# Conformer/attention encoder layer on one core: branches stored as two halves, score products chunk by chunk, and the convolution norm in seventeen short steps

## The chip, the cores and the metric

One core of a Trainium2 chip runs the whole kernel in one launch. The metric is the device time of one launch in microseconds (us). The profile is one execution taken by the hardware profiler; its times are counted from the first instruction of that execution.

## The reference, cut to what matters

One encoder layer, on a prompt of 1024 tokens and a sample of 256 tokens, which the kernel lays side by side as T = 1280 columns (features on the 128 partitions, in blocks of 128). Everything is float32.

```
h = modulate(rms_norm(x), sh1, sc1)                       # sh, sc, g: from silu(c) @ w_ada + b_ada
c_q, c_kv, k_r, conv_in, sg_in, gate_in = split(h @ w_in)
y_attn = attention(c_q, c_kv, k_r) @ w_attn_o             # 8 heads, softmax over all keys of the sequence
y_conv = silu(layer_norm(depthwise_conv31(glu(conv_in)))) @ w_conv_o    # 512 channels
y_sg   = (u * (spatial mix of layer_norm(v))) @ w_sg_o                  # 512 channels
x = x + g1 * ((ga*y_attn + gc*y_conv + gs*y_sg) @ w_out)  # ga, gc, gs = sigmoid(gate_in)
x = x + g2 * conv_ffn(modulate(rms_norm(x), sh2, sc2))
```

The layer norm of the convolution branch runs over 512 channels, that is over four blocks of 128 partitions. Its mean and its variance are sums over partitions, made on TensorE by products with a matrix of ones.

## The kernel before, in words

**Products.** Nearly all products are made three times, from operands split into a high part (`hi`, rounded to fp32r) and a low part (`lo`, the rest): hi times hi, hi times lo, lo times hi (`mm3`, line 130). `to_hi` (L117) makes the high part on GpSimd (POOL in the profile), `to_lo` (L120) subtracts on VectorE (DVE). `split` (line 142) does both on a [128, 1280] tile. Weights are loaded by SyncE (SP), split by the same two engines, and held up to three jobs ahead (`run_jobs`).

**Jobs and side steps.** The work is a list of jobs, each of which writes its instructions in program order. Beside them runs a queue `side` of short steps; `run_side(n)` writes the next n of them between two jobs. A scheduler then sorts each engine's instructions: it takes them in program order as they become ready by its own estimate, so an engine with nothing ready may take up later work, and an instruction that is ready goes ahead of everything later in the program. On the chip each engine, and each queue of transfers (SP's and POOL's), then runs strictly in the order that came out.

**The stretch around the change.** 24 gate jobs (`gate`, line 640), each one block of `h @ w_in` with a sigmoid on ScalarE (ACT, L643) and a store to `gate_d`. Behind gate 16 the side queue is emptied; then it gets the convolution norm as one step (`conv_norm`, line 322) and the 16 blocks of conditioning (`ada_steps`: start, `ada_blk` 0 to 15 on VectorE at L663, end). Behind each of the gates 17 to 23 run three side steps, 19 in all. `end_one` writes what is left, gives the tiles of `h` back, and attention follows (`attention`, line 747): it takes four output tiles `ob`, then loads head 0 with `load_head` (five transfers of 640 KB on POOL's queue, L726 and L729: q hi, q lo, k hi, k lo, v), and then goes through 72 units of scores (L736), softmax (L741 to L744), transposes (L801) and products with v (L818). Each next head is loaded two units into the head before; in head 7 the place of the next head is taken by `branch_load(us_d)`, which loads the four blocks of the gated branch and splits them. After attention come 24 jobs `branch_out`, and with the second of these `branch_load(cn_d)`, the same for the convolution branch. Both branches were stored to DRAM as they are, one tile per block: `us_d` by `sgu` (L421), `cn_d` by `conv_norm` (L350).

**The norm as one step.** `conv_norm` loads the four blocks (L326), adds them (L328 on POOL, L329 and L330 on DVE), makes the mean in three column chunks with a product by ones (L333, tile `pcm`) and subtracts it out of PSUM on DVE (L335, twelve instructions); then squares (L337 to L340), variance (L344, tile `pcv`), `rsqrt_big` (L149 and L151 to L154 on DVE, L150 on ACT), and for each block a product with the inverse (L348, every second one on POOL), silu (L349) and a store. The pool `sm` that holds `pcm` and `pcv` has two buffers.

**The slots.** All big tiles (1280 columns) come from 33 slots. The list of free slots is first in, first out, fixed when the program is written, and each slot is a buffer of its own:

```
def take(self, dt=F32, w=SLOTW):
    i = self.free.popleft()
    ...
    t = self.pool.tile([P, w], dt, name=f"t{self.n}", tag=f"s{i}")
def drop(self, *ts):
    ...
        self.free.append(i)
```

The first instruction that writes a newly taken tile waits until the last one that read or wrote the tile that had the slot before is done; where that was a store, until the store has landed.

## Time and profile before

| what | value |
|---|---|
| median of 3 runs | 2137.91 us (2137.29 to 2138.53) |
| the profiled execution, its own time | 2137.02 us |
| its span, first to last instruction | 2135.3 us |
| TensorE (PE) busy | 2076.5 us, 97% of the span |
| VectorE (DVE) busy | 1447.7 us, 68% |
| ScalarE (ACT) busy | 821.3 us, 38% |
| GpSimd (POOL) busy | 601.8 us, 28% |
| mean granted TensorE clock | 0.992 of full |

How to read it: an engine's time is the time in which one of its instructions runs. The rows of a timeline give the start in us, the duration in us, engine, line of the kernel, operation, the tiles written and read, the number of instructions merged into the row, and in square brackets how long the engine sat idle just before and what ended that. A row `DMA_DIRECT2D` under SP or POOL is the issue of a transfer; its landing is shown apart. A merged row runs from the start of its first instruction to the end of its last.

### The profile page before, as it was taken

How to read it: one execution, taken by the hardware profiler on the slowest of the kernel's cores; microseconds unless marked ns; L12 is line 12 of the kernel's file. 1: busy time of each engine (PE TensorE's matmuls, PEld its weight loads, DVE VectorE, ACT ScalarE, POOL GpSimd, SP SyncE). 2: the span in 40 equal slices, each digit the busy share in tenths (PEclk: the TensorE clock that was granted, in tenths of full speed). 3: DMA queues.
4: the chain of work that ended last, by engine and by line, in shares of the span. 5: the costliest groups of instructions: out<-in, count | busy, mean ns of one | idle time of the engine just before them, and what ended most of it. 6: DMA issues, size and time to landing. Idle time of an engine off the chain costs nothing. (4 is left out here: it accounts for less than half of the span.)

```text
span 2135.3 us, 29511 instructions
## 1 busy us (share of the span) xinstructions
PE 2076.5 (97%) x11094; PEld 1768.9 (83%) x11094; DVE 1447.7 (68%) x2151; ACT 821.3 (38%) x1637; POOL 601.8 (28%) x460
## 2 busy tenths in 40 slices
PE   6999999999999999999999998999999999999999
PEld 2888888887887788887888877888888888788889
DVE  6969798545447588888786398766666666644344
ACT  5110130345433177762000165544444444533233
POOL 2302202232312144452133432444444443000000
PEclk9999999999999999999999999999999999999999
DMA  8102232457685733326635322232223323856455
GB/s 340 49 23 80 91 112 83 144 176 223 186 278 181 233 104 113 106 100 254 216 139 193 106 99 71 95 96 95 84 85 94 94 84 104 261 176 199 136 172 162
DMA packets 146544, 300.82 MB, mean 141 GB/s; under 512 B 12129, under 2 KB 69601, under 8 KB 146401
## 3 DMA queue, kind: packets, MB, share of 16 engines
q1 hardware_dynamic: 136032, 254.37, 35.5%
q0 software_dynamic: 10368, 44.57, 6.7%
q8 instruction: 87, 1.43, 0.3%
q14 instruction: 57, 0.46, 0.1%
HBM read 220.24 MB, written 78.64 MB: 140 GB/s over the span
## 5 line engine op out<-in xcount | busy, mean ns | idle before, releaser
L1125 PE MATMUL b<-t,wq 128*128 128x512 f32 (+1 forms) x2904 | 551.9, 352 | 9.2 <-ACT t L1045 4.2
L1125 PEld LDWEIGHTS b<-t,wq 128*128 128x128 f32 x2904 | 474.9, 190 | 86.6 <-ACT t L1045 4.6
L139 PE MATMUL pb<-t,whi 128*128 128x512 f32 (+1 forms) x1632 | 443.4, 358 | 0.0
L120 DVE TENSOR_TENSOR wq<-wst,wq 128x512 fp32r<-128x512 f32 x308 | 247.4, 812 | 182.4 <-ACT wq L989 181.0
L139 PEld LDWEIGHTS pb<-t,whi 128*128 128x128 f32 x1632 | 289.2, 190 | 41.4 <-POOL whi L117 0.2
L1249 PE MATMUL pd<-t,wq 128*128 128x512 f32 (+1 forms) x1584 | 302.9, 354 | 0.0
L1249 PEld LDWEIGHTS pd<-t,wq 128*128 128x128 f32 x1584 | 261.7, 189 | 41.2
L989 ACT ACTIVATE wq<-wst 128x512 fp32r<-128x512 f32 x308 | 193.0, 630 | 260.1 <-PE pd L1249 70.5
L139 PE MATMUL pb<-t,wlo 128*128 128x512 f32 (+1 forms) x816 | 290.7, 356 | 0.0
L117 POOL TENSOR_SCALAR whi<-wst 128x1024 fp32r<-128x1024 f32 (+1 forms) x76 | 96.3, 1267 | 412.1 <-PE pb L139 184.7
L139 PE MATMUL bp<-t,whi 128*128 128x512 f32 x640 | 200.3, 393 | 2.9 <-DVE t L120 2.9
L120 DVE TENSOR_TENSOR t<-t,t 128x512 fp32r<-128x512 f32 (+4 forms) x139 | 135.0, 992 | 89.6 <-ACT t L1208 67.0
L294 DVE SCALAR_TENSOR_TENSOR t<-t,col,t 128x1009 f32<-128x1009 f32 (+14 forms) x240 | 194.2, 876 | 0.0
L139 PEld LDWEIGHTS pb<-t,wlo 128*128 128x128 f32 x816 | 154.8, 190 | 21.2
L120 DVE TENSOR_TENSOR wlo<-wst,whi 128x1024 fp32r<-128x1024 f32 (+1 forms) x76 | 82.4, 1086 | 113.6 <-POOL whi L117 103.3
L139 PEld LDWEIGHTS bp<-t,whi 128*128 128x128 f32 x640 | 118.8, 189 | 27.5 <-DVE t L120 4.1
L139 PE MATMUL bp<-t,wlo 128*128 128x512 f32 x320 | 125.1, 391 | 0.0
L736 PE MATMUL ps<-t,t 128*128 128x512 f32 (+1 forms) x432 | 113.6, 396 | 4.0 <-ACT t L742 2.5
L117 POOL TENSOR_SCALAR t<-t 128x1280 fp32r<-128x1280 f32 (+3 forms) x37 | 79.2, 2151 | 135.0 <-DMA t<-in_wqkv 59.9
L1183 POOL TENSOR_TENSOR t<-t,t 128x1280 f32<-128x1280 f32 x22 | 73.4, 3335 | 155.7 <-ACT wq L989 116.1
L744 POOL TENSOR_SCALAR t<-t,sz 128x1024 f32<-128x1024 f32 (+1 forms) x80 | 82.4, 1030 | 119.4 <-DVE sz L743 107.8
L643 ACT ACTIVATE t<-pb 128x1280 f32<-128x1280 f32 x24 | 29.8, 1243 | 206.6 <-PE pb L139 199.5
(198 smaller groups left out, 2870.8 us busy)
## 6 DMA issues: line engine op xcount, KB each, us to landing
wst<-in_wup SPq DMA_DIRECT2D x66, 512.0 KB, 3.6
wst<-in_wdn SPq DMA_DIRECT2D x132, 256.0 KB, 2.9
t<-in_ada SPq DMA_DIRECT2D x48, 512.0 KB, 6.3
qk_d<-t SPq DMA_DIRECT2D x80, 256.0 KB, 3.3
t<-qk_d POOLq DMA_DIRECT2D x32, 640.0 KB, 4.7
wst<-in_win SPq DMA_DIRECT2D x36, 512.0 KB, 4.1
gate_d<-t SPq DMA_DIRECT2D x24, 640.0 KB, 3.3
t<-gate_d SPq DMA_DIRECT2D x24, 640.0 KB, 5.3
```

Source lines behind the costliest of these rows:

```text
L117: G.tensor_scalar(out=out, in0=in_, scalar1=1.0, scalar2=0.0, op0=ALU.mult, op1=ALU.add)
L120: V.tensor_tensor(out=out, in0=in_, in1=hi.bitcast(F32), op=ALU.subtract)
L139: PE.matmul(ps.at(o, n) if isinstance(ps, Two) else ps[:, o:o + n], ws[:, c:c + P], ms[:, s:s + n], start=first and j == 0 and q == 0, sto ...
L294: V.scalar_tensor_tensor(out=ac[:, o + a:o + e], in0=ci[:, o + a + d:o + e + d], scalar=w, in1=ac[:, o + a:o + e], op0=ALU.mult, op1=ALU.add)
L643: S.activation(out=gt, in_=ps[:, :T], func=AF.Sigmoid)
L736: PE.matmul(ps[:, o + c:o + c + w], qk[a][:, q0:q0 + P], qk[b][:, k0 + c:k0 + c + w], start=q == 0, stop=q == 2)
L744: G.tensor_scalar(out=pr[:, o:o + n], in0=pr[:, o:o + n], scalar1=z[:, 2:3], scalar2=0.0, op0=ALU.mult, op1=ALU.add)
L989: S.activation(out=w[:, :HB], in_=src, func=AF.Copy)
L1125: PE.matmul(ps, w[:, c + k * P:c + (k + 1) * P], bs[k][i], start=start and k == 0 and q == 0, stop=stop and k == 3 and q == 2, skip_group_ ...
L1183: G.tensor_tensor(out=c["y1"], in0=c["y1"], in1=y2, op=ALU.mult)
L1249: PE.matmul(pss[m][:, :n], w[:, a + m * P:a + (m + 1) * P], t[:, b:b + n], start=k == 0 and q == 0, stop=k == KF - 1 and q == 2)
```

## The change

- `us_d` and `cn_d` get a second plane. `sgu` splits its result at once (`put`: POOL to_hi, DVE to_lo, two stores instead of one). `conv_norm` makes the two halves at its end, the high one on ACT. `branch_load` then only loads eight tiles, on POOL's queue instead of SP's, and splits nothing.
- `scores` goes chunk by chunk (512 keys): the three products of a chunk one behind the other, instead of both chunks for each of the three.
- `conv_norm` no longer writes instructions at once. It hands 17 steps to the side queue: load, sums, mean of three chunks, centre of four blocks, squares, variance of three chunks, four blocks. The first sum moves from POOL to DVE; the mean goes from PSUM to SBUF by an ACT copy and is then subtracted from whole blocks; the four products with the inverse are all on DVE.
- The order behind gate 16 is turned round: first the conditioning (18 steps with start and end), then the norm (17 steps). Five side steps instead of three run behind each of the gates 17 to 23, 35 in all. The last five, behind gate 23, are the variance of the third chunk and the four blocks.

```diff
@@ -104,9 +104,9 @@
         return col[:, at + i:at + i + n]
 
     gate_d = dr.tile([3, KD, P, T], F32, name="gate_d")
-    us_d = dr.tile([4, P, T], F32, name="us_d")
+    us_d = dr.tile([4, 2, P, T], F32, name="us_d")
     ac_d = dr.tile([4, P, T], F32, name="ac_d")
-    cn_d = dr.tile([4, P, T], F32, name="cn_d")
+    cn_d = dr.tile([4, 2, P, T], F32, name="cn_d")
     lat_d = dr.tile([NT, P, 6 * P], F32, name="lat_d")
     qk_d = dr.tile([2, 2, H, P, T], F32, name="qk_d")
     v_d = dr.tile([H, P, NT, P], F32, name="v_d")
@@ -144,6 +144,12 @@
         to_hi(h[:, :width], src[:, :width])
         to_lo(l[:, :width], src[:, :width], h[:, :width])
         return h, l
+
+    def put(dst, src):
+        hl = split(src)
+        for p in range(2):
+            SY.dma_start(dst[p], hl[p].bitcast(F32))
+        sl.drop(*hl)
 
     def rsqrt_big(y, ps, o, n, scale, s, t):
         V.tensor_scalar(out=s[:, o:o + n], in0=ps, scalar1=scale, scalar2=EPS, op0=ALU.mult, op1=ALU.add)
@@ -320,36 +326,60 @@
         job(lambda: run_side(n))
 
     def conv_norm():
-        acc = []
-        for b in range(4):
-            acc.append(sl.take())
-            SY.dma_start(acc[b], ac_d[b])
-        t1, t2 = sl.take(), sl.take()
-        G.tensor_tensor(out=t1, in0=acc[0], in1=acc[1], op=ALU.add)
-        V.tensor_tensor(out=t2, in0=acc[2], in1=acc[3], op=ALU.add)
-        V.tensor_tensor(out=t1, in0=t1, in1=t2, op=ALU.add)
-        for o, n in CH3:
+        acc, t, u = [], [], []
+
+        def load():
+            for b in range(4):
+                acc.append(sl.take())
+                SY.dma_start(acc[b], ac_d[b])
+            t.extend((sl.take(), sl.take()))
+
+        def sums():
+            V.tensor_tensor(out=t[0], in0=acc[0], in1=acc[1], op=ALU.add)
+            V.tensor_tensor(out=t[1], in0=acc[2], in1=acc[3], op=ALU.add)
+            V.tensor_tensor(out=t[0], in0=t[0], in1=t[1], op=ALU.add)
+
+        def mean(o, n):
             ps = sm.tile([P, 512], F32, name="pcm", tag="sm")
-            PE.matmul(ps[:, :n], ones, t1[:, o:o + n], start=True, stop=True)
-            for b in range(4):
-                V.scalar_tensor_tensor(out=acc[b][:, o:o + n], in0=ps[:, :n], scalar=-1.0 / 512,
-                                       in1=acc[b][:, o:o + n], op0=ALU.mult, op1=ALU.add)
-        S.activation(out=t1, in_=acc[0], func=AF.Square)
-        for b in range(1, 4):
-            S.activation(out=t2, in_=acc[b], func=AF.Square)
-            V.tensor_tensor(out=t1, in0=t1, in1=t2, op=ALU.add)
-        y, t3 = sl.take(), sl.take()
-        for o, n in CH3:
+            PE.matmul(ps[:, :n], ones, t[0][:, o:o + n], start=True, stop=True)
+            S.activation(out=t[1][:, o:o + n], in_=ps[:, :n], func=AF.Copy, scale=1.0 / 512)
+
+        def centre(b):
+            V.tensor_tensor(out=acc[b], in0=acc[b], in1=t[1], op=ALU.subtract)
+
+        def squares():
+            S.activation(out=t[0], in_=acc[0], func=AF.Square)
+            for b in range(1, 4):
+                S.activation(out=t[1], in_=acc[b], func=AF.Square)
+                V.tensor_tensor(out=t[0], in0=t[0], in1=t[1], op=ALU.add)
+
+        def var(o, n):
+            if not u:
+                u.extend((sl.take(), sl.take()))
             ps = sm.tile([P, 512], F32, name="pcv", tag="sm")
-            PE.matmul(ps[:, :n], ones, t1[:, o:o + n], start=True, stop=True)
-            rsqrt_big(y, ps[:, :n], o, n, 1.0 / 512, t2, t3)
-        sl.drop(t1, t2, t3)
-        for b in range(4):
-            (G if b % 2 else V).tensor_tensor(out=acc[b], in0=acc[b], in1=y, op=ALU.mult)
+            PE.matmul(ps[:, :n], ones, t[0][:, o:o + n], start=True, stop=True)
+            rsqrt_big(u[0], ps[:, :n], o, n, 1.0 / 512, t[1], u[1])
+
+        def block(b):
+            if b == 0:
+                sl.drop(*t, u.pop())
+            V.tensor_tensor(out=acc[b], in0=acc[b], in1=u[0], op=ALU.mult)
             S.activation(out=acc[b], in_=acc[b], func=AF.Silu, scale=cv("clg", b), bias=cv("clb", b))
-            SY.dma_start(cn_d[b], acc[b])
-            sl.drop(acc[b])
-        sl.drop(y)
+            h_, l_ = sl.take(F32R), sl.take(F32R)
+            S.activation(out=h_, in_=acc[b], func=AF.Copy)
+            to_lo(l_, acc[b], h_)
+            SY.dma_start(cn_d[b, 0], h_.bitcast(F32))
+            SY.dma_start(cn_d[b, 1], l_.bitcast(F32))
+            sl.drop(acc[b], h_, l_)
+            if b == 3:
+                sl.drop(u.pop())
+
+        side.extend((load, sums))
+        side.extend([lambda c=c: mean(*c) for c in CH3])
+        side.extend([lambda b=b: centre(b) for b in range(4)])
+        side.append(squares)
+        side.extend([lambda c=c: var(*c) for c in CH3])
+        side.extend([lambda b=b: block(b) for b in range(4)])
 
 
     wv, vg = [], []
@@ -418,7 +448,7 @@
                 scalar=cv("sgg", g), in1=tt[:, g * P:(g + 1) * P].unsqueeze(1).to_broadcast([P, NT, P]),
                 op0=ALU.mult, op1=ALU.add)
             V.tensor_tensor(out=us, in0=us, in1=u, op=ALU.mult)
-            SY.dma_start(us_d[g], us)
+            put(us_d[g], us)
             sl.drop(us, u)
             if g == 3:
                 sl.drop(wst, tt, *vg)
@@ -705,10 +735,10 @@
             job(lambda: run_side(4))
         elif j == 16:
             job(lambda: run_side(len(side)))
-            job(lambda: side.append(conv_norm))
             job(lambda: ada_steps(range(16)))
+            job(conv_norm)
         else:
-            job(lambda: run_side(3))
+            job(lambda: run_side(5))
 
     def end_one():
         run_side(len(side))
@@ -730,9 +760,9 @@
         return r, t
 
     def scores(ps, o, qk, q0, k0, n):
-        for q, (a, b) in enumerate(((0, 2), (0, 3), (1, 2))):
-            for c in range(0, n, 512):
-                w = min(512, n - c)
+        for c in range(0, n, 512):
+            w = min(512, n - c)
+            for q, (a, b) in enumerate(((0, 2), (0, 3), (1, 2))):
                 PE.matmul(ps[:, o + c:o + c + w], qk[a][:, q0:q0 + P], qk[b][:, k0 + c:k0 + c + w],
                           start=q == 0, stop=q == 2)
 
@@ -845,10 +875,10 @@
     def branch_load(src):
         r = []
         for b in range(4):
-            st = sl.take()
-            SY.dma_start(st, src[b])
-            r.append(split(st))
-            sl.drop(st)
+            hl = sl.take(F32R), sl.take(F32R)
+            for p in range(2):
+                G.dma_start(hl[p], src[b, p])
+            r.append(hl)
         return r
 
     job(attention)
```

## Rows read from the trace of the kernel before

**Rows 1.** The page's first lines: the span, and TensorE's busy time with its share of the span and the number of its instructions, products and weight loads.

```profile
span 2135.3 us, 29511 instructions
PE 2076.5 (97%) x11094; PEld 1768.9 (83%) x11094; DVE 1447.7 (68%) x2151; ACT 821.3 (38%) x1637; POOL 601.8 (28%) x460
```

**Rows 2.** The timeline of DVE, PE and ACT in the stretch of the gates 17 to 23: the sum of the four blocks, the three mean products, and the sigmoids at the ends of the gates 17, 18, 22 and 23.

```profile
624.77 1.49 DVE L330 TENSOR_TENSOR t<-t,t 128x1280 f32<-128x1280 f32 x1
...
645.25 1.88 PE L333 MATMUL pcm<-t,ones 128*128 128x512 f32 x4
652.68 1.12 PE L333 MATMUL pcm<-t,ones 128*128 128x256 f32 x2 [2.34 <-DVE t L335]
...
645.45 1.24 ACT L643 ACTIVATE t<-pb 128x1280 f32<-128x1280 f32 x1 [12.43 <-PE pb L139]
...
665.66 1.24 ACT L643 ACTIVATE t<-pb 128x1280 f32<-128x1280 f32 x1 [2.13 <-PE pb L139]
...
723.14 1.24 ACT L643 ACTIVATE t<-pb 128x1280 f32<-128x1280 f32 x1 [12.54 <-PE pb L139]
736.92 1.24 ACT L643 ACTIVATE t<-pb 128x1280 f32<-128x1280 f32 x1 [12.53 <-PE pb L139]
```

**Rows 3.** Busy time by stretch, two pieces of 5 us behind the mean products: from left the stretch, its length, busy us and instructions of PE, of its weight loads, DVE, ACT and POOL, the granted clock, the DMA share and GB/s.

```profile
650.00:655.00 5.00, 2.66 (x8) 1.85 (x7) 5.00 (x10) 0.00 (x0) 0.00 (x0) 0.78 0.86 313
655.00:660.00 5.00, 5.00 (x21) 4.04 (x20) 2.83 (x6) 3.01 (x3) 0.00 (x0) 0.88 0.05 21
```

**Rows 4.** The timeline where attention starts: the end of a conditioning block (DVE), the first of head 0's loads (POOL), the first scores (PE) and the first softmax (ACT).

```profile
705.36 0.23 DVE L665 TENSOR_SCALAR ada<-ada,col 128x2 f32<-128x2 f32 x1
...
705.84 0.60 POOL L726 DMA_DIRECT2D t<-qk_d  x1 [9.21 <-DVE ada L665]
...
738.21 3.06 PE L736 MATMUL ps<-t,t 128*128 128x512 f32 x12 [1.33 <-ACT t L643]
743.77 4.49 PE L736 MATMUL ps<-t,t 128*128 128x512 f32 x12 [2.50 <-ACT t L742]
...
741.21 1.28 ACT L742 ACT_TABLE_LOAD   x1 [3.06 <-DVE sz L741]
```

**Rows 5.** The timeline of DVE and ACT in the norm itself: the addition of a square on 1280 columns, a 256-column step of the inverse root, the two table loads, the inverse root on ACT, and the four silus.

```profile
663.57 1.49 DVE L340 TENSOR_TENSOR t<-t,t 128x1280 f32<-128x1280 f32 x1 [1.34 <-ACT t L339]
...
674.47 0.42 DVE L151 SCALAR_TENSOR_TENSOR t<-t 128x256 f32<-128x256 f32 x1
...
668.89 1.28 ACT L150 ACT_TABLE_LOAD   x1 [1.99 <-DVE t L149]
670.18 1.46 ACT L150 ACTIVATE t<-t 128x512 f32<-128x512 f32 x3
671.66 1.28 ACT L349 ACT_TABLE_LOAD   x1
682.23 5.63 ACT L349 ACTIVATE t<-t,col 128x1280 f32<-128x1280 f32 x4 [9.28 <-POOL t L348]
```

**Rows 6.** Transfers of one 640 KB tile, all of the kernel: what is moved, the issuing queue, count, size and median us from issue to landing.

```profile
us_d<-t SPq DMA_DIRECT2D x4, 640.0 KB, 3.1
cn_d<-t SPq DMA_DIRECT2D x4, 640.0 KB, 5.3
t<-us_d SPq DMA_DIRECT2D x4, 640.0 KB, 5.4
t<-qk_d POOLq DMA_DIRECT2D x32, 640.0 KB, 4.7
```

**Rows 7.** The same from 595 to 760 us only, head 0's and head 1's v; and, as busy time by stretch (columns as in rows 3), the 5 us from 595 to 745 us in which the transfers were fastest, while `cn_d` was stored.

```profile
t<-v_d POOLq DMA_DIRECT2D x2, 640.0 KB, 7.2
685.00:690.00 5.00, 5.00 (x23) 4.13 (x22) 4.97 (x5) 4.96 (x5) 3.36 (x2) 1.00 1.00 403
```

**Rows 8.** The timeline of attention's end: PE at the ninth unit of the heads 5, 6 and 7, DVE's splits of the gated branch, and the transposes that came after them.

```profile
903.56 0.53 PE L736 MATMUL ps<-t,t 128*128 128x256 f32 x3
...
931.93 0.52 PE L736 MATMUL ps<-t,t 128*128 128x256 f32 x3
...
965.55 0.52 PE L736 MATMUL ps<-t,t 128*128 128x256 f32 x3
...
942.34 6.12 DVE L120 TENSOR_TENSOR t<-t,t 128x1280 fp32r<-128x1280 f32 x3
...
950.25 1.11 PE L801 MATMUL ptt<-ident,t 128*128 128x128 f32 x4 [4.16 <-DVE t L779]
```

**Rows 9.** The timeline of the gated branch (`sgu`), 172 to 246 us: a weight's high half on POOL twice, and DVE waiting for one; then the last split of the weights that the next stage needs, and ACT's first instruction of that stage. Last, the whole stretch 174 to 240 us (columns as in rows 3).

```profile
204.94 6.00 POOL L117 TENSOR_SCALAR whi<-wst 128x1024 fp32r<-128x1024 f32 x1 [11.30 <-issue]
228.86 1.05 POOL L117 TENSOR_SCALAR whi<-wst 128x1024 fp32r<-128x1024 f32 x1
...
243.01 1.85 DVE L120 TENSOR_TENSOR t<-t,t 128x832 fp32r<-128x832 f32 x1 [7.61 <-POOL t L117]
...
255.34 0.49 ACT L452 ACTIVATE t<-psl 128x384 f32<-128x384 f32 x1 [17.08 <-PE psl L449]
174.00:240.00 66.00, 66.00 (x372) 57.80 (x371) 55.19 (x60) 6.37 (x6) 25.61 (x6) 1.00 0.30 102
```

**Rows 10.** Groups by line and shape, TensorE: the scores and the gates' products on 512 columns, count, busy us, mean ns of one.

```profile
L736 PE MATMUL ps<-t,t 128*128 128x512 f32 x384 | 105.6, 408 | 3.8 <-ACT t L742 2.5 <-ACT t L643 1.3
L139 PE MATMUL pb<-t,whi 128*128 128x512 f32 x1088 | 344.7, 395 | 0.0
```

## The prediction, made before the changed kernel was run

> **What bounds the kernel now.** First the page: TensorE is busy for 97% of the span, the others far less, and it makes as many weight loads as products [rows 1]. So the end is set by TensorE's work plus the few tens of us in which it has nothing to do, and an edit that leaves its products alone is worth what it takes from or adds to those holes. Next I listed who makes TensorE wait, and looked at the timeline of each place that the change touches. There are three.
>
> *The mean products behind gate 17.* The third mean product waits 2.34 us for DVE [rows 2]: `sm` has two buffers, and DVE empties them in twelve instructions. Behind it the granted clock falls: 0.78 and 0.88 in two pieces of 5 us [rows 3]. With 1.2 and 2.4 GHz as its levels that is 2.2 and 1.2 us at the low one, 1.7 us of work lost. Gate 18's sigmoid comes 20.2 us after gate 17's; a gate's pace is 13.78 us [rows 2], and the mean products need about 2.5 us. Lost: 3.9 us, which agrees with 2.34 + 1.7.
>
> *The end of attention.* The ninth units of the heads 5 and 6 lie 28.37 us apart, those of the heads 6 and 7 33.62 us [rows 8]. In between DVE splits the gated branch for 6.12 us on end, and transposes wait 4.16 us [rows 8]. Lost: 5.25 us.
>
> *The start of attention.* Gate 23's sigmoid begins at 736.92, so its products end there (call it G), and the scores begin 1.3 us later [rows 2, 4]. That works because head 0 was loaded early: its first load goes out at 705.84, released by a conditioning block [rows 4], two gates before the end. Why that block? The slots. At the end of the gates the free list holds, oldest first, what the last gates and conditioning blocks gave back; `ob` takes four, head 0 the next five. Counting takes and drops backwards by hand, head 0's first tile gets the slot of block 9's weights, and block 9 is done at 705.6 [rows 4]. So the list decides when the loads start.
>
> **The change, part by part.** The sum is made against the profiled execution, 2137.0 us, 0.9 us under the median of the runs.
>
> *The order behind gate 16.* 35 steps at five per gate: the steps behind gate 23 are the variance of chunk three and the four blocks. The variance is a product on TensorE. Can the scheduler bring it forward? In the kernel before, the sum of the blocks was done at 626.3, and the mean product, written behind gate 17, ran at 645.25, right behind gate 17 [rows 2]. A product written later waits for the gate's products, which are always ready. So nothing of the last five steps starts before G, while the conditioning of the kernel before ran ahead.
>
> Now the slots. Before gate 23 there are 24 in use: 16 of `h`, four blocks, two sums, two of the inverse. Nine are free, the last of them gate 23's own tile after its store. Block 0 drops three and takes two for its halves; each block drops itself and its halves. At the start of attention the list reads: gate 23's tile, the three dropped by block 0 (these four go to `ob`), then block 0, its hi, its lo, block 1, its hi. These five are head 0. So q hi waits for block 0's split, q lo and k hi for the stores of block 0's halves to land, k lo for block 1's split. POOL's queue holds them in order, with nothing to do for TensorE behind them but attention.
>
> The path from G, with durations of such instructions: sigmoid of gate 23, 1.24 [rows 2]; table load, 1.28, and inverse root on 256 columns, 0.4, an estimate from 1.46 for 1280 [rows 5]; the variance product and its evacuation lie under these. Now 2.9. Three DVE steps of 0.42: 4.2. Product with the inverse, 1.49: 5.7. Silu, 1.24 (its table load lies under the DVE steps; measured 5.63 for four [rows 5]): 6.9. High half on ACT, as long: 8.2. Low half, as long as an addition: 9.7. Store of the low half, 5.3 as `cn_d` took: 15.0. Load of k hi: 7.2, the v loads' time in this stretch [rows 7]: 22.2. So the scores start 22.2 instead of 1.3 after G: **+20.9**. From below: the store lands in 3.1 as `us_d` did, the load in 4.7 [rows 6], 17.5 after G: +16.2. From above: eight stores and four loads, 7.9 MB, share the engines at 403 GB/s, the fastest stretch [rows 7]; 19.5 us from 8.2 on make 27.7, +26.4. I take the middle one, because the stores come as close together as the four of `cn_d` did.
> On the table loads the Trainium skill (ScalarE: Activation LUTs, What ACT_TABLE_LOAD costs) counts a drain of about 1.4 us with each; by it the term would be 22.3. The row has ACT's next instruction 0.01 us behind the load [rows 5], so the sum goes without it.
>
> *The mean.* Moved behind gate 21, it leaves PSUM by one ACT copy per chunk instead of four DVE steps. What is late next is the third product, behind gate 21's sigmoid on ACT: some tenths. **-3.5**, between -3.9 and 0 (0 if the variance products, which now fall into gate 23's stream, wait as the mean did). The rest of the norm runs under gates. DVE's extra sum and POOL's relief touch nothing that TensorE waits for.
>
> *The splits of the gated branch* leave attention: **-5.3**. What comes instead is eight loads on POOL's queue at 0.60 us of issue each [rows 4], against four splits. Behind them wait softmax steps, needed three units later, some 9 us at 28.37 us per nine units [rows 8]. If the loads' slots come late they take some back: -5.3 to -2. The convolution branch's splits lie under `branch_out`, where TensorE did not wait for them: 0.
> A rule against this part: by the Trainium skill (SBUF — State Buffer, SBUF: two separate sides) a transfer issued from GpSimd can starve while DVE holds the shared port; its figures, 0.62 us alone and 3.1 beside DVE, would make this term about -2.8. The rows disagree: POOL's loads of heads landed in 4.7 us in the midst of attention, SP's of `us_d` in 5.4 [rows 6].
>
> *The split in `sgu`* adds, four times, POOL's high half, DVE's low half and a store. TensorE was busy in all 66 us there, with DVE 10.8 and POOL 40 us idle [rows 9]. DVE's four low halves need 5.9, plus waits for POOL, which takes 6.00 instead of 1.05 beside DVE [rows 9]. The cover is slack: the next stage's weights are split at 244.9 and its first result is out at 255.3 [rows 9]. I take 0; +4 if lateness reaches that stage, nothing below.
>
> *Scores by chunk.* Each product keeps its own weight load [rows 1], and the reduction reads both chunks at once: 0. From below: 408 ns against 395 for the gates' products [rows 10], times 384, -5.0; from above 0. I take 0, since the scores' mean holds the slow starts.
>
> *Restart.* After 20 idle us the first scores run at a low clock: twelve took 4.49 instead of 3.06 when slow [rows 4]; the old start paid this once too. **+0.5**, 0 to +2.
>
> Sum: 20.9 - 3.5 - 5.3 + 0.5 = +12.6, so 2149.6. With all lower bounds 16.2 - 3.9 - 5.3 - 5.0 = +2.0; all upper ones together (+30.4) are not to be expected.
>
> **The rivals.** *Head 0 is not held up* (faster): the place is gate 23, the price the 20.9 us. It decides if the last five steps get ahead of gate 23's products in the scheduler's estimate, or if the loads go to slots free for long. Then only the savings count: 2137.0 - 8.8 = 2128.2. For it: engines do take up later work when idle. Against it: the mean product that did not get ahead [rows 2], and a slot count that hits the old first load to 0.3 us [rows 4]. 0.12.
> *The delay is half hidden* (no change): the norm's DVE and ACT steps pass faster, or scores begin on early tiles; a start about 10 us after G gives +8.8 - 8.8: 2137.0. Against it: k hi hangs on a store, and three instructions, a store and a load alone exceed it. 0.07.
> *Transfers pile up* (slower still): stores and loads as from above, 26.4, and the mean's saving lost to new waits: 26.4 - 5.3 + 0.5 = +21.6, 2158.6. For it: two 640 KB stores per 2.5 us of ACT are 520 GB/s, more than 403 [rows 7]. 0.16.
> *Forecast*: 0.65, by itself 2142 to 2156.
>
> **How the numbers follow.** A measurement of this kernel tells about 0.2%, 4.3 us, from no change. The forecast and the third rival are slower by more than that: 0.81. The second is the same. The first is faster. The range leaves the first out and most of the second, and reaches over the third with its bounds: 2140 to 2161.
>
> **What would show it.** In the changed profile: a hole of 16 to 26 us in TensorE between the variance's third product and the first L736, with POOL waiting in its loads of `qk_d` for DVE's low halves and `cn_d` stores, where TensorE was busy before; the ninth units of the heads 6 and 7 about 28.4 us apart; gates 17 to 23 at 13.8 us but for the small products. The forecast is wrong if head 0's loads go out before gate 23's end.

## The result, and the profile of the changed kernel

The changed kernel takes 2153.53 us (median of 4 runs, 2151.49 to 2156.70), the kernel before 2138.19 beside it: ratio 1.0083 [1.007, 1.0096]. It is slower, by 15 us; the forecast was 2149.6, its range 2140 to 2161. The profiled execution took 2156.70 us, the slowest of its four, with a span of 2154.9.

TensorE's busy time is that of before within 1.1 us, and the span is 19.6 us longer [rows 1]:

```profile
span 2154.9 us, 29529 instructions
PE 2075.4 (96%) x11094; PEld 1767.8 (82%) x11094; DVE 1451.7 (67%) x2146; ACT 826.9 (38%) x1645; POOL 578.1 (27%) x469
```

So the time went into holes. TensorE's waits in the whole kernel, the longest group first (us in total, times, longest):

```profile
PE ps L766 <- DMA t<-qk_d: 30.8, 1, 30.8
```

The scores (now L766) wait for the planes of head 0; before, TensorE's list of waits had none for `qk_d`. The start of attention in the timeline: gate 23's sigmoid (L673), the norm's products with the inverse (L366), the silus with their table load (L367), copies (L369) and low halves (L120), the first and the last store (L371, L372), head 0's four loads of planes (L756) and the first scores.

```profile
733.35 1.24 ACT L673 ACTIVATE t<-pb 128x1280 f32<-128x1280 f32 x1 [8.98 <-PE pb L139]
...
737.72 5.70 DVE L366 TENSOR_TENSOR t<-t,t 128x1280 f32<-128x1280 f32 x4
...
739.29 1.28 ACT L367 ACT_TABLE_LOAD   x1 [2.98 <-DVE t L366]
740.59 2.80 ACT L367 ACTIVATE t<-t,col 128x1280 f32<-128x1280 f32 x2
743.29 2.41 ACT L369 ACTIVATE t<-t 128x1280 fp32r<-128x1280 f32 x2
...
744.58 2.89 DVE L120 TENSOR_TENSOR t<-t,t 128x1280 fp32r<-128x1280 f32 x2 [1.16 <-ACT t L369]
...
744.57 0.33 SPq L371 DMA_DIRECT2D cn_d<-t  x1
...
752.97 0.64 SPq L372 DMA_DIRECT2D cn_d<-t  x1
...
746.36 0.60 POOL L756 DMA_DIRECT2D t<-qk_d  x1 [12.47 <-DVE t L120]
747.77 1.06 POOL L756 DMA_DIRECT2D t<-qk_d  x2 [0.81 <-DVE t L120]
749.77 0.53 POOL L756 DMA_DIRECT2D t<-qk_d  x1 [0.94 <-issue]
...
764.52 4.37 PE L766 MATMUL ps<-t,t 128*128 128x512 f32 x12 [30.77 <-DMA t<-qk_d]
```

The reader is to see two stretches. From the sigmoid to the issue of the last load of planes, 749.77 - 733.35 = 16.4 us, the norm's blocks pass through ACT, DVE and SP. From there to the scores, 14.75 us, TensorE waits for that load; ACT and DVE end their blocks in the first 3 us of it, and then hardly anything but transfers runs. These keep the DMA engines busy all the time and move 403 to 415 GB/s (columns as in rows 3; the clock granted to TensorE is at the lower level, 0.50):

```profile
752.00:756.00 4.00, 0.00 (x0) 0.00 (x0) 0.48 (x1) 0.14 (x1) 1.06 (x2) 0.50 1.06 403
...
760.00:764.00 4.00, 0.00 (x0) 0.00 (x0) 0.00 (x0) 0.00 (x0) 0.67 (x2) 0.50 1.07 415
```

Transfers issued from 740 to 770 us (count, size, median us to landing), where before the medians had been 5.3 for `cn_d` and 4.7 to 7.2 for the loads [rows 6, 7]:

```profile
cn_d<-t SPq DMA_DIRECT2D x8, 640.0 KB, 9.0
t<-qk_d POOLq DMA_DIRECT2D x8, 640.0 KB, 11.9
t<-v_d POOLq DMA_DIRECT2D x1, 640.0 KB, 15.4
```

The two gains came. Gate 17's sigmoid, the mean products, and the ninth units of the heads 6 and 7 (against [rows 2, 8]):

```profile
646.34 1.25 ACT L673 ACTIVATE t<-pb 128x1280 f32<-128x1280 f32 x1 [12.54 <-PE pb L139]
...
701.25 1.88 PE L344 MATMUL pcm<-t,ones 128*128 128x512 f32 x4
703.23 0.70 PE L344 MATMUL pcm<-t,ones 128*128 128x256 f32 x2
...
957.07 0.53 PE L766 MATMUL ps<-t,t 128*128 128x256 f32 x3
...
985.61 0.52 PE L766 MATMUL ps<-t,t 128*128 128x256 f32 x3
```

The balance, profiled execution against profiled execution: gate 23's sigmoid 733.35 for 736.92, -3.6; the scores 31.2 us behind it for 1.3, +29.9; first scores to the ninth unit of head 0, 23.15 us for 24.27, -1.1; heads 6 to 7, 28.54 for 33.62, -5.1. Sum +20.1; the spans differ by 19.6.

In one profile G is uncertain by some 4 us. Gates 7 to 10, which the edit does not touch, took 66.75 us here at a mean granted clock of 0.95, 64.81 at 0.97 in the profile of before, and 62.05 at 1.00 in that of e2 below, with 321 products each time; in the two longer ones TensorE waited there once for over 2 us for DVE before the clock fell, in e2 for 1.6 at most. The mean's gain is better read from gate 17's sigmoid to gate 23's: 87.01 us for 91.47, -4.5. Of this 0.6 is the third variance product, which now runs behind G; the rest, 3.9, is the mean's.

### The profile page after: what moved, and what is told of

The parts are those of the page before. It is cut to its first block, busy times and chain, and to the rows that moved or that the text cites. A ratio compares the mean times of both kernels' runs of the same rounds, so it can differ in the third digit from the quotient of the medians.

```text
span 2154.9 us, 29529 instructions
## 1 busy us (share of the span) xinstructions
PE 2075.4 (96%) x11094; PEld 1767.8 (82%) x11094; DVE 1451.7 (67%) x2146; ACT 826.9 (38%) x1645; POOL 578.1 (27%) x469
## 5 line engine op out<-in xcount | busy, mean ns | idle before, releaser
L120 DVE TENSOR_TENSOR wq<-wst,wq 128x512 fp32r<-128x512 f32 x308 | 247.5, 812 | 179.5 <-ACT wq L1019 178.2
L300 DVE SCALAR_TENSOR_TENSOR t<-t,col,t 128x1009 f32<-128x1009 f32 (+14 forms) x240 | 202.5, 902 | 0.0
L120 DVE TENSOR_TENSOR t<-t,t 128x512 fp32r<-128x512 f32 (+4 forms) x139 | 131.7, 966 | 87.7 <-ACT t L1238 67.5
L120 DVE TENSOR_TENSOR wlo<-wst,whi 128x1024 fp32r<-128x1024 f32 (+1 forms) x76 | 81.4, 1072 | 122.6 <-POOL whi L117 112.4
L766 PE MATMUL ps<-t,t 128*128 128x512 f32 (+1 forms) x432 | 112.8, 394 | 32.1 <-DMA t<-qk_d 30.8
L673 ACT ACTIVATE t<-pb 128x1280 f32<-128x1280 f32 x24 | 29.8, 1243 | 223.6 <-PE pb L139 223.6
L766 PEld LDWEIGHTS ps<-t,t 128*128 128x128 f32 x432 | 74.5, 191 | 47.6 <-issue 31.1
```

Of the source, the lines that this page charges most:

```text
L120: V.tensor_tensor(out=out, in0=in_, in1=hi.bitcast(F32), op=ALU.subtract)
L300: V.scalar_tensor_tensor(out=ac[:, o + a:o + e], in0=ci[:, o + a + d:o + e + d], scalar=w, in1=ac[:, o + a:o + e], op0=ALU.mult, op1=ALU.add)
L673: S.activation(out=gt, in_=ps[:, :T], func=AF.Sigmoid)
L766: PE.matmul(ps[:, o + c:o + c + w], qk[a][:, q0:q0 + P], qk[b][:, k0 + c:k0 + c + w], start=q == 0, stop=q == 2)
```

## The experiments

**Theory A**: head 0's planes take the slots that the last side steps give back, so their loads wait for those steps, and then share the DMA engines with the steps' eight stores. **Rival B**: ACT's and DVE's tail of blocks would hold the softmax about as long, even with the planes there. **Rival C**: the loads are slow by themselves, or held by something ahead of them on POOL's queue.

From each kernel's timeline: G (start of gate 23's sigmoid), the first scores, the ninth unit of head 0, the distance of the ninth units of the heads 6 and 7, and the span of the profiled execution; the ratio is that of all runs, its interval stands with each experiment. (In e9 one of the ninth unit's three products ran ahead, at 756.16; the time is that of the other two, which elsewhere run with it.)

| kernel | G | scores | ninth | 6 to 7 | span | ratio to before |
|---|---|---|---|---|---|---|
| before | 736.92 | 738.21 | 762.48 | 33.62 | 2135.3 | 1 |
| changed | 733.35 | 764.52 | 787.67 | 28.54 | 2154.9 | 1.0083 |
| e1 norm first | 730.38 | 745.51 | 774.50 | 28.54 | 2140.6 | 1.0033 |
| e2 `ob` last | 729.48 | 742.30 | 774.04 | 28.52 | 2140.1 | 1.0028 |
| e3 six steps | 734.84 | 746.95 | 777.28 | 28.53 | 2144.0 | 1.0044 |
| e4 fewer stores | 733.07 | 759.88 | 783.40 | 28.55 | 2150.0 | 1.0062 |
| e3b seven steps | 735.52 | 746.31 | 774.61 | 28.54 | 2140.9 | 1.0036 |
| e7 early head | 730.19 | 731.48 | 772.19 | 28.53 | 2140.5 | 1.0023 |
| e8 seven, early | 740.30 | 741.59 | 764.90 | 28.52 | 2130.5 | 0.9978 |
| e5 branches only | 744.72 | 746.01 | 770.66 | 28.53 | 2137.2 | 1.0013 |
| e11 norm steps only | 733.11 | 734.40 | 766.40 | 33.40 | 2138.4 | 1.0012 |
| e6 scores only | 737.86 | 739.15 | 763.40 | 33.39 | 2136.1 | 0.9998 |
| e10 load first | 734.23 | 735.52 | 762.96 | 28.54 | 2130.0 | 0.9993 |
| e9 mixed | 730.34 | 731.63 | 759.31 | 28.53 | 2126.7 | 0.9958 |

### What holds the planes of head 0

e1, the norm ahead of the conditioning:

```
+            job(conv_norm)
             job(lambda: ada_steps(range(16)))
-            job(conv_norm)
```

> The changed kernel with the two groups of side steps in the other order: first the 17 steps of the norm, then the 18 of the conditioning; five per gate as before. Theory A (slots and queues: head 0's five tiles take the slots that the last five side steps give back, so its loads wait for whatever runs last): the last steps are conditioning blocks, the loads go out before gate 23 ends, the 30.8 us hole shrinks to 1 to 3 us and the other savings stay (3.6 at the mean, 5.1 at the end of attention): 2126 to 2131 us. Rival B (ScalarE and VectorE are still busy with the norm when attention starts): the same here, since the norm is over by then. Rival C (the loads are slow by themselves, or were put behind something else in GpSimd's queue by the change): the hole stays at 25 us or more, 2148 us or more.

2142.81 us, 1.0033 [1.002, 1.0045]: over half of the loss is gone, yet the expectation missed, since a hole of 15 us stays. It has another last user. POOL's first load of head 0, and the scores:

```profile
733.41 0.60 POOL L756 DMA_DIRECT2D t<-qk_d  x1 [1.59 <-DVE ada L695]
...
745.51 1.19 PE L766 MATMUL ps<-t,t 128*128 128x512 f32 x2 [15.17 <-DMA t<-qk_d]
```

Now the conditioning is what ends last (`ada`, L695), and head 0 takes its slots: for A. It is late because its loads follow the norm's stores in SP's order; DVE waited for them (`t<-in_ada`):

```profile
710.36 1.23 DVE L693 SCALAR_TENSOR_TENSOR t<-t,t 128x1024 f32<-128x1024 f32 x1 [6.26 <-DMA t<-in_ada]
```

e2, head 0 taken before `ob`, so that it gets the four oldest free slots:

```
+        heads = {0: load_head(0)}
         ob = [sl.take() for _ in range(4)]
         kept["ob"] = ob
-        heads = {0: load_head(0)}
```

> The changed kernel with one line moved: attention takes the five tiles of head 0 before the four of ob. The work and the order of the side steps are unchanged; only which slots head 0 gets. Theory A: q hi, q lo, k hi, k lo then get the slots of gate 23's tile and of the three scratch tiles of the norm; these are free 4 to 6 us behind gate 23, before any store of cn_d, so the loads land about 12 us behind gate 23 and the hole falls from 30.8 to 10 to 13 us: about 2135 us if nothing else holds attention up. Rival B: the scores start early as well, but the first softmax waits for the last block on VectorE and ScalarE, some 19 us behind gate 23, so that a second hole takes half of it back: 2140 to 2146 us. Rival C: the hole stays at 25 us or more, 2148 us or more.

2142.12 us, 1.0028 [1.0016, 1.0039], about as expected. One line moved, and 9.5 of the 15.3 us came back; the work is the same. The wait for planes fell to 13.2 us, in two pieces (A had 10 to 13), and behind it a second hole opened for ACT, which is B's part, hidden in the changed kernel; with it the time is the one that B named:

```profile
742.30 1.19 PE L766 MATMUL ps<-t,t 128*128 128x512 f32 x2 [12.43 <-DMA t<-qk_d]
744.24 4.63 PE L766 MATMUL ps<-t,t 128*128 128x512 f32 x10 [0.75 <-DMA t<-qk_d]
754.17 5.32 PE L766 MATMUL ps<-t,t 128*128 128x512 f32 x12 [5.29 <-ACT t L772]
```

e4 takes load off the DMA engines: blocks 2 and 3 of the normalised branch are not stored, and the planes of the blocks 0 and 1 are loaded in their place.

```
-            SY.dma_start(cn_d[b, 0], h_.bitcast(F32))
-            SY.dma_start(cn_d[b, 1], l_.bitcast(F32))
+            if b < 2:
+                SY.dma_start(cn_d[b, 0], h_.bitcast(F32))
+                SY.dma_start(cn_d[b, 1], l_.bitcast(F32))
...
-                G.dma_start(hl[p], src[b, p])
+                G.dma_start(hl[p], src[b if src is us_d else b % 2, p])
```

> The changed kernel in which blocks 2 and 3 of the convolution branch are not stored, and block 0's and 1's planes are loaded in their place: four of the eight stores of 640 KB at the end of the norm are left out, and those that head 0's slots wait for stay. Theory A with transfers that pile up: 2.6 MB less at about 410 GB/s, so up to 6.4 us off the landing of head 0's last tile; the hole falls from 30.8 to 24 to 27 us, 2146 to 2150 us. If head 0 waits for the slots and the latency of a store and a load alone, not for the bandwidth: the hole stays within 2 us of 30.8, 2151 to 2156 us.

2149.03 us, 1.0062 [1.0048, 1.0075]; the wait is 4.4 us shorter, as expected:

```profile
759.88 4.85 PE L767 MATMUL ps<-t,t 128*128 128x512 f32 x12 [26.41 <-DMA t<-qk_d]
```

Stores that are issued beside or behind head 0's loads delay them: the four left out come last in the row. The 4.4 us is less than four stores cost, since head 1's four planes, issued up to 766.04 in the changed kernel, are all out by 753.89 here and take part of the room.

e3 and e3b end the side steps earlier, with six or seven of them a gate:

```
-            job(lambda: run_side(5))
+            job(lambda: run_side(6))      # e3; 7 in e3b
```

> The changed kernel with six side steps behind each gate instead of five, so that the last five steps of the norm come behind gate 22 and not behind gate 23. Theory A: nothing changes in the chain from the third variance product to head 0's loads, but it starts one gate (13.8 us) earlier, and gate 23 covers so much of it: the hole falls from 30.8 to 15 to 18 us, 2136 to 2140 us. Rival C: the hole does not follow the place of the steps and stays at 25 us or more.

> The changed kernel with seven side steps a gate alone, head 0 taken where the change takes it. Theory A: the last side step gives its tiles back some 16 us earlier than with six (e3, hole 20.3 us), so that head 0's loads are issued before gate 23's sigmoid: hole 0 to 5 us, 2127 to 2134 us. If the hole comes from the loads themselves or from what stands ahead of them on POOL (C), it stays over 10 us: 2137 or more.

2146.04 us, 1.0044 [1.0028, 1.006], and 2144.36, 1.0036 [1.0023, 1.0048]: both missed, in size: the holes are 20.3 and 12.75 us. In e3b the fourth load of planes goes out at 731.4, before G at 735.5, as A has it, and still the scores wait:

```profile
731.44 0.53 POOL L756 DMA_DIRECT2D t<-qk_d  x1 [1.04 <-DMA cn_d<-t]
...
746.31 1.19 PE L766 MATMUL ps<-t,t 128*128 128x512 f32 x2 [10.83 <-DMA t<-qk_d]
749.42 4.06 PE L766 MATMUL ps<-t,t 128*128 128x512 f32 x10 [1.92 <-DMA t<-qk_d]
```

Again 15 to 18 us from that issue to the use. The transfers issued from 718 to 750 us are the norm's stores, the loads of two heads and two gates' stores, all slow together:

```profile
cn_d<-t SPq DMA_DIRECT2D x8, 640.0 KB, 9.7
t<-qk_d POOLq DMA_DIRECT2D x8, 640.0 KB, 11.4
t<-v_d POOLq DMA_DIRECT2D x2, 640.0 KB, 11.0
gate_d<-t SPq DMA_DIRECT2D x2, 640.0 KB, 16.0
```

So A's second half, the sharing, by itself still makes 12.75 of the 30.8 us. An earlier start moves the heap of transfers; it does not thin it.

e7 asks for head 0's tiles behind gate 20, long before the stores; e8 does so with seven steps a gate:

```
             job(lambda: run_side(5))      # 7 in e8
+            if j == 20:
+                job(lambda: kept.update(h0=load_head(0)))
...
-        heads = {0: load_head(0)}
+        heads = {0: kept.pop("h0")}
```

> The changed kernel, but head 0's five tiles are taken and its loads issued behind the side steps of gate 20, when nine tiles have long been free, instead of behind the last side step. Theory A (the 30.8 us before the first scores are tile slots given back late by the last side steps, and then loads and stores sharing the DMA engines): the wait of the first scores for the qk planes falls from 30.8 to under 2 us. What is left is the ACT and DVE tail of the blocks behind gate 23, which holds the first softmax some 10 to 13 us: 2134 to 2142 us. If the loads were slow by themselves (C), the wait for the planes stays over 10 us. If the ACT tail costs nothing (against B): 2126 to 2131.

> As e7, and seven side steps a gate in place of five, so that the last block of the normalised branch is through behind gate 21 and no step is left behind gate 23. Theory A with B: neither the wait for planes nor the wait of the first softmax for ACT is left (under 3 us together), the mean's gain and the 5 us at the end of attention stay: 2126 to 2131 us, faster than both kernels. Rival: seven steps a gate hold up the gates' own sigmoids and products, so that gate 23 ends over 4 us later than in the changed kernel: 2132 to 2140.

e7: 2142.04 us, 1.0023 [1.0014, 1.0031], just past the range of A. The scores follow gate 23 at once, so C falls: the same loads, issued early into free slots and away from the stores, are no hindrance. The second scores then wait for ACT longer than I gave B, 18 us:

```profile
731.48 3.01 PE L768 MATMUL ps<-t,t 128*128 128x512 f32 x12 [0.89 <-ACT t L673]
752.66 4.97 PE L768 MATMUL ps<-t,t 128*128 128x512 f32 x12 [18.17 <-ACT t L774]
```

The blocks' silus and copies fill ACT from 739.5 to 749.7 there, ahead of the first exponential. So two holes lay on top of each other, and the longer one hid the other.

e8: 2131.85 us, 0.9978 [0.9967, 0.9988], a little over the range; neither hole is left (the second scores wait 2.50 us for ACT, as before [rows 4]), and it is faster than both kernels. But G came at 740.30, 10 us later than in e7. This is not what the rival named, sigmoids that wait on ACT behind the norm: they do come late (one at 733.21, 23.4 us behind the one before), but TensorE works on meanwhile. 2 of the 10 us lie ahead of gate 17. The other 8 lie between 672.81 and 694.71, two sigmoids 21.9 us apart. There the mean products waited 5.2 us for the sum of the four blocks, the last of which was asked for only at 667.59, and behind the wait the granted clock was 0.50 for 4 us and 0.79 for 4 more:

```profile
PE pcm L344 <- DVE t L340: 5.2, 1, 5.2
```

### The parts alone

e5 is the kernel before with the branches' planes only (`put`, the norm's stores by halves, `branch_load`):

> The kernel before with only the branches stored as hi and lo and loaded by halves (us and cn); the norm, its place and the scores as before. Prediction's term: the splits at the end of attention leave, -5.3 us (bounds -5.3 to -2): 2131 to 2134 us beside 2136.3. Rival: the doubled stores and loads (5 MB more through the queues) hold up head 0 or the softmax steps: 2136 to 2142.

2139.85 us, 1.0013 [1.0004, 1.0022]: a miss, though the 5 us at the end of attention are there (28.53). The time lies in the rival's range, but not by its mechanism: head 0 and the softmax are not held up. The cost is on ACT. Before, gate 18's sigmoid ran at 665.66, ahead of the norm's silus [rows 2, 5]; here ACT's order has the sigmoids of both gate 18 and gate 19 behind all silus and the four copies (4.8 us), and they run one after the other at 685.89. `pb` has two buffers, and TensorE stands 12 us until the first of the two sigmoids is done:

```profile
682.17 2.42 ACT L357 ACTIVATE t<-t 128x1280 fp32r<-128x1280 f32 x2
684.60 1.28 ACT L653 ACT_TABLE_LOAD   x1
685.89 2.37 ACT L653 ACTIVATE t<-pb 128x1280 f32<-128x1280 f32 x2
...
687.23 1.19 PE L139 MATMUL pb<-t,whi 128*128 128x512 f32 x2 [11.87 <-issue]
```

e11 is the kernel before with the norm's steps only, one plane per block:

```
-            h_, l_ = sl.take(F32R), sl.take(F32R)
-            S.activation(out=h_, in_=acc[b], func=AF.Copy)
-            to_lo(l_, acc[b], h_)
-            SY.dma_start(cn_d[b, 0], h_.bitcast(F32))
-            SY.dma_start(cn_d[b, 1], l_.bitcast(F32))
-            sl.drop(acc[b], h_, l_)
+            SY.dma_start(cn_d[b], acc[b])
+            sl.drop(acc[b])
```

> The kernel before with only the norm in short steps behind the conditioning, five steps a gate; branches in one plane and scores as before. Theory A: the last step's slots are still what head 0 waits for, with four stores and four copies fewer than in the changed kernel (e4's four stores were worth 4.4 us, the copies 4.8 of ACT), so the wait of the first scores is 18 to 24 us in place of 30.8; the mean gains 3.6, the end of attention keeps its splits: 2148 to 2156 us. If the doubled stores alone made the wait (C): 2131 to 2136.

2139.99 us, 1.0012 [1.0003, 1.0021]: a miss for both theories as I put them. No wait for planes at all: head 0's four planes are out by 722.20, before G, because the blocks take no slots for halves, and eight more takes do not push head 0 to the end of the list.

```profile
674.96 1.14 POOL L746 DMA_DIRECT2D t<-qk_d  x2 [13.27 <-ACT t L663]
709.46 0.58 POOL L746 DMA_DIRECT2D t<-qk_d  x1 [7.67 <-DMA gate_d<-t]
722.20 0.58 POOL L746 DMA_DIRECT2D t<-qk_d  x1 [3.35 <-DMA gate_d<-t]
...
741.18 1.28 ACT L361 ACT_TABLE_LOAD   x1 [0.74 <-DVE t L360]
742.47 5.49 ACT L361 ACTIVATE t<-t,col 128x1280 f32<-128x1280 f32 x4
747.98 1.28 ACT L762 ACT_TABLE_LOAD   x1
...
734.40 3.01 PE L756 MATMUL ps<-t,t 128*128 128x512 f32 x12 [0.89 <-ACT t L663]
```

What it pays is B's part: between the first exponentials ACT does the four silus with a table load on either side, and from G to the ninth unit it takes 33.3 us in place of 25.6.

e6 is the kernel before with the scores by chunk only:

> The kernel before with only the scores chunk by chunk. Prediction's term: 0 us, bounds -5 to 0: 2132 to 2137 us beside 2136.8. Rival: the weight loads, now changed at each matmul, show: over 2139.

2135.94 us, 0.9998 [0.999, 1.0007]; 408 ns a product, as before [rows 10]:

```profile
L736 PE MATMUL ps<-t,t 128*128 128x512 f32 x384 | 105.8, 408 | 3.8 <-ACT t L742 2.5 <-ACT t L643 1.3
```

The parts alone give +0.13, +0.12 and -0.02%, together 0.23%, some 5 us; all at once cost 0.83%. The rest, about 13 us, belongs to none of them: it needs the halves, with their slots and their stores, and the late steps together. That it is the slots in the first place follows from the list and from e2 and e11; no run splits these 13 us further.

### A version that beats both

e9 takes up what e7 and e8 left: head 0 behind gate 20, six steps a gate, and the norm's 17 steps in turn with the conditioning's 18, so that its loads go early and its blocks are spread. (The expectation puts part of e8's delay down to the blocks; by the profile above it was the late sum.)

```
             job(conv_norm)
+            job(mix)      # one step of the norm, one of the conditioning, and so on
         else:
-            job(lambda: run_side(5))
+            job(lambda: run_side(6))
+            if j == 20:
+                job(lambda: kept.update(h0=load_head(0)))
```

> The changed kernel with head 0 taken and its loads issued behind gate 20's side steps (as e7), six side steps a gate, and the norm's 17 steps handed out in turn with the conditioning's 18 from gate 17 on, so that its loads are early and its blocks are spread. Theory (in e8 the gates were held 10 us: 8 by the late loads of the accumulator, which ACT's squares waited for, and the rest by four blocks in a row ahead of a sigmoid; in e7 head 0's softmax was held 18 us by blocks still behind gate 23): gate 23's sigmoid at 730 to 734 us, first scores within 2 us of it, no wait over 3 us for ACT at the second scores, the end of attention as in the changed kernel: 2122 to 2128 us. If the blocks still hold the gates or the softmax: 2130 to 2136.

2127.92 us, 0.9958 [0.9946, 0.997], as expected but for the wait at the second scores, 4.30 in place of under 3. First scores, second scores, and the transfers issued from 655 to 735 us, each row well under the 9.0 and 11.9 us of the changed kernel, at 205 GB/s over the stretch:

```profile
731.63 3.04 PE L779 MATMUL ps<-t,t 128*128 128x512 f32 x12 [1.33 <-ACT t L673]
738.97 4.62 PE L779 MATMUL ps<-t,t 128*128 128x512 f32 x12 [4.30 <-ACT t L785]
```

```profile
cn_d<-t SPq DMA_DIRECT2D x8, 640.0 KB, 5.8
t<-qk_d POOLq DMA_DIRECT2D x5, 640.0 KB, 4.8
```

e10 leaves the blocks in a row and moves the norm's load step alone to the front:

```
             job(conv_norm)
+            job(lambda: side.appendleft(side[18]))
+            job(drop_19)
```

> As e9, but the conditioning's steps ahead of the norm's, with the norm's load step alone moved to the front: the four blocks come in a row behind gates 21 and 22. Theory: the loads' wait (8 us in e8) is gone, what the row of blocks holds stays, 4 to 10 us between the gates' sigmoids or at the first softmax: 2126 to 2134 us. If only the late loads held the gates in e8: as e9, 2122 to 2128.

2136.69 us, 0.9993 [0.9983, 1.0002], a miss. Its runs lie in two heaps, around 2132 (4 of 12) and around 2137, and the profiled one is of the lower (span 2130.0). In that one the sigmoids of gates 17 to 20 are 13.8 us apart, so with early loads and six steps e8's 21.9 us are gone. What the row of blocks costs is a wait of 4.54 us at the first scores: gate 23's sigmoid (734.23) stands behind all four blocks on ACT. What the upper heap loses was not seen. A candidate is gates 7 to 10, which take 62.05 us in this profile and up to 4.7 us more in others (see the result); it stays open.

## Why the prediction was right, step by step

**The start of attention, +20.9: right in kind, mis-sized, +29.9.** The chain is the predicted one: variance, four blocks, slots, loads, with POOL waiting for DVE's low halves. The last plane's load went out 16.4 us after G where the prediction had 15.0, and that it came so close is partly luck. Block 0's low half was ready at 12.7 instead of 9.7: the silu's table load did not lie under the DVE steps, it came behind the first product (739.29), and ACT ran silus and copies by twos, so that block 1's silu stood ahead of block 0's copy. Its store then landed in 3.1 us instead of 5.3, as the first stores met little else.

What failed is the last leg: the load of the last plane, set at 7.2 us, took 14.6. The 7.2 was taken from a stretch in which head loads met few stores, and the sharing was kept for a rival; that eight stores and the loads would go as the four stores of `cn_d` had gone was the step that did not hold. e4 shows that leaving out four of the eight stores takes 4.4 us off, e3b that 15 us stay when loads and stores start earlier together, e9 that loads away from the stores land in 4.8. Even the bound from above, 26.4, was too low, and so the hole, 30.8 us, lies outside the 16 to 26 that the prediction gave as its sign. The bound's rate was not the fault: its twelve tiles at 403 GB/s make 19.5 us, and 19.95 passed from the first store to the scores. But the first store went out 11.2 us after G, not 8.2; and the bytes were not those of the twelve tiles. By then 7.4 MB had been moved, the last two stores were still under way (they landed at 765.6 and 768.7), and `v` and head 1's first plane had shares of their own.

With its largest term 9 us short in the profile the forecast still came within 3.9 us of the median, 2153.5 for 2149.6: the profiled execution is 3.2 us above the median, and the other terms came out 2.0 lower in sum. The range held because it reached over the pile-up.

**The slots: right.** e2, which only changes who takes first, moved the wait as the list had said. e11, which takes eight fewer, fits the list too, but only afterwards: its expectation had counted head 0 into the last steps' slots.

**The mean, -3.5: right** (-3.9 between gates 17 and 23, no wait at the third product). **The splits, -5.3: right** (-5.1; eight loads on POOL cost nothing that TensorE shows). **`sgu`, 0: right**; TensorE is busy in all 72 us from 172 to 244 us (below; columns as in rows 3). **Scores by chunk, 0: right**; e6 is its direct measure. **Restart, +0.5**: the first twelve took 4.37 us instead of 3.06, but the stretch to the ninth unit got 1.1 shorter. The softmax's table load ran in the hole (755.86), so that the second scores waited 1.08 us for ACT instead of 2.50 and took 3.20 instead of 4.49 [rows 4].

```profile
172.00:244.00 72.00, 72.00 (x409) 63.19 (x408) 69.90 (x68) 7.48 (x6) 20.16 (x11) 1.00 0.37 132
```

**The rivals.** The pile-up is what mis-sized the forecast; its time of 2158.6 assumed that the mean's saving would be lost, and it was not. Head 0 not held up, 2128.2, was brought about by hand in e9, and 2127.9 was measured, but by another sum: G 6.6 us earlier (2.7 of them in gates 7 to 10), the ninth unit 3.4 us later behind G, and the 5.1 at the end of attention. What the prediction did not see is the hole behind the hole: with the planes there in time, ACT's blocks hold the first softmax for 18 us (e7).

## What to carry to other kernels

When a pool hands out its slots oldest first, every take that a step adds moves all later takes to younger slots: count the takes between the change and the next urgent load, not only the work. Price a load that starts beside a burst of stores by all the bytes in flight, those of other queues and of later loads included, over the measured rate, and place it ahead of the burst. When a hole has two causes, ask for each how long it would last alone (e2, e7), since the removal of the longer one uncovers the other.

## What the runs showed of the hardware

Loads issued by POOL and stores issued by SP slow each other: 640 KB landed in medians of 4.8 to 5.8 us with the engines partly free (e9, 205 GB/s in sum), and of 9 to 16 us while they moved 396 to 416 GB/s in sum (the changed kernel from 752 us on, e3b from 726). The Trainium skill (DMA: Bandwidth & Descriptors, Queues, rings and completion order) says that an engine goes round between its queues packet by packet; the trace agrees in that both queues moved on at the same pace: in the changed kernel loads landed at 753.5, 757.6, 761.3 and 764.4, stores at 755.8, 759.3, 762.4 and 765.6 us. That the turns go packet by packet no run here shows.

In the changed kernel TensorE stood still from 733.8 us on; it was granted 0.50, the level of 1.2 GHz, from 738 to 766, and the first twelve products took 4.37 us; at the higher level they take 3.0 (e7). Where two functions alternate on ACT, table loads add to its work: in e11 the four silus between exponentials took 5.49 us, and the two table loads around them 2.6 more.
